# Three eighths of the first feed-forward product as seven block products, in a written sequence

## The chip, the cores and the metric

One core of one Trainium2 chip runs the whole kernel. The metric is device time in microseconds (us) of one execution. Engines: TensorE (PE) multiplies, VectorE (DVE) and ScalarE (ACT) prepare and evict, GpSimd (POOL) does little, SyncE (SP) issues the loads. Each engine takes its instructions in the order in which they stand in its own queue; semaphores tie the queues together.

## The reference

A residual block of a streaming encoder: a retention branch and a latent-attention branch, merged by gates, then a squared-ReLU MLP. Everything is float32; 256 rows (SEQ), model width 2048, hidden width 8192. The change touches the MLP alone:

```python
z = _rmsnorm(h, norm_mlp_g[l]) @ w_up[l]          # 256 x 2048 by 2048 x 8192
h = h + jnp.square(jax.nn.relu(z)) @ w_down[l]    # 256 x 8192 by 8192 x 2048
return _rmsnorm(h, norm_f_g)
```

## The kernel before

Every float32 operand is split in two float32r halves, `hi` (ScalarE rounds it, L151 for weights, L216 or L219 for activations) and `lo = raw - hi` (VectorE, L152, L217 or L220). A product is the sum of hi·hi, hi·lo and lo·hi in PSUM. Weights arrive by SyncE in 512 KB tiles `raw` (five buffers), and give `hi` and `lo` (four buffers each).

There are two forms of product. A *transposed unit* (`t_unit`, L170) holds a 128 x 128 block of weights stationary and streams the activations: for each of 16 blocks along the contraction one matmul of 512 columns (L159: x hi and x lo side by side) and one of 256 (L163: weight lo by x hi). Its 128 outputs by 256 rows lie in one PSUM bank in two halves, which `joined` adds (L206 copies one half by ScalarE, L207 adds by VectorE). The *normal form* (`n_tile`, L196, and `down`, L807) holds the activations stationary and streams 512 columns of weights, three matmuls for each block: L199, L200, L202, or L814, L815, L816.

The MLP runs in three stages. In the stage `wo` (L770) the merged branches are multiplied with `w_out`; 512 columns at a time are added to `hn`, and `mlp_turn` (L757) transposes them through PSUM (L764) and splits them into `hT`. In the stage `up` (L785 to L800) 64 transposed units give `z`; L800 squares the positive part into `hid`, which stays in SBUF. In the stage `dn` (L802 to L838) each of 64 blocks of `hid` is split into `dh` and `dl` (three buffers each, L820 to L822) and multiplied with two 512 KB halves of `w_down` into eight PSUM banks; L840 to L863 add, normalise and store.

PSUM has eight banks of 512 float32 columns, four under the tag `mm` and four under `at`. Within a stage the order of the instructions on each engine is set by the framework's scheduler from costs that it assumes; the program's order is only its input.

Of the kernel before, what the change touches and what calls it, by code (L numbers as in the profile page):

```python
# [27 lines left out]
CHUNK = 64  # L28
DFF = 8192
FT = DFF // P  # L30
EPS = 1e-6
QK_SCALE = float(192.0 ** -0.5)
LOWEST = -3.4e38
# [55 lines left out]
def block_kernel(ctx: ExitStack, tc: tile.TileContext, A):  # L89
    nc = tc.nc  # L90
    V, SC, G, PE = nc.vector, nc.scalar, nc.gpsimd, nc.tensor
# [3 lines left out]
    cp = ctx.enter_context(tc.tile_pool(name="cp", bufs=1))  # L95
# [4 lines left out]
    def big(name, dt=F32, shape=(P, KT, S)):  # L100
        return act.tile(list(shape), dt, tag="act16", name=name)
# [31 lines left out]
    def mmps(name):  # L133
        return pmm.tile([P, 512], F32, tag="mm", name=name)
# [4 lines left out]
    uid = [0]  # L139
# [15 lines left out]
    HK = KT // 2  # L155
# [40 lines left out]
    def n_tile(out, w, x, t, k0, nk, start, stop):  # L196
# [4 lines left out]
        for k in range(nk):  # L201
            PE.matmul(out, x.hi(k0 + k, ts), w[1][:, k], start=False, stop=stop and k == nk - 1)  # L202

    def join(out, ps):
        t = sm.tile([P, S], F32, tag="join", bufs=2, name="join")
        SC.copy(t, ps[:, S:])  # L206
        V.tensor_tensor(out=out, in0=ps[:, :S], in1=t, op=ALU.add)  # L207

    def joined(ps):
        t = sm.tile([P, S], F32, tag="val", bufs=2, name="val")  # L210
        join(t, ps)
        return t

    def split(hi, lo, val, scale=None):
        if scale is None:
            SC.copy(hi, val)  # L216
            V.tensor_tensor(out=lo, in0=val, in1=hi.bitcast(F32), op=ALU.subtract)  # L217
# [12 lines left out]
    warm = cp.tile([P, 1], F32, name="warm")  # L230
    SC.activation(warm, halfpi, AF.Copy)

    cold = cp.tile([P, 512], BF16, name="cold")
# [5 lines left out]
    rctx = ExitStack()  # L239
    rope_pool = rctx.enter_context(tc.tile_pool(name="rope", bufs=2))  # L240
    ictx = ExitStack()
    ip = ictx.enter_context(tc.tile_pool(name="ip", bufs=1))

# [8 lines left out]
    x = Pair("x")  # L252
# [97 lines left out]
    rxb = cp.tile([P, S], F32, name="rxb")  # L350
    V.tensor_copy(rxb, pb[:, :S])

    tabs = []
# [1 line left out]
    def table(j):  # L355
        ang, kk = angs[j]
        sgn = vec[:, V_INV + 2 + j : V_INV + 3 + j]
        own = ip if j == 0 else cp
        cos = own.tile([P, S], F32, name=f"cos{j}")
        sin = own.tile([P, S], F32, name=f"sin{j}")  # L360
# [157 lines left out]

    with ExitStack() as mctx:
        cc = big("cc", F32R, shape=(P, 2 * LT, 2, S))  # L520
        kpe = cp.tile([P, S], F32, name="kpe")
        lp = ExitStack()
        lpool = lp.enter_context(tc.tile_pool(name="lp", bufs=1))

# [230 lines left out]
    hT = Pair("hT")  # L755

    def mlp_turn(c):  # L757
        for jj in range(2):
            pT = atps(f"ht{c}{jj}")
            for j in range(2):  # L760
                kt = 4 * c + 2 * jj + j
                for t in range(2):
                    o = j * S + t * P
                    PE.transpose(pT[:, o : o + P], hn[:, t, kt * P : (kt + 1) * P], ident)  # L764
                g = vec[:, V_MLP + kt : V_MLP + kt + 1]
                split(hT.hi(kt), hT.lo(kt), pT[:, j * S : (j + 1) * S], scale=g)
    hp = ctx.enter_context(tc.tile_pool(name="hp", bufs=1))
    ssh = cp.tile([P, 2, 4], F32, name="ssh")
    rh2 = cp.tile([P, 2], F32, name="rh2")
    for c in range(4):  # L770
        cs = slice(c * 512, (c + 1) * 512)
        pss = [mmps(f"wo{c}{t}") for t in range(2)]
        for kq in range(4):
            n_unit(pss, A["w_out"][4 * c + kq], mg, 4 * kq, 4, kq == 0, kq == 3)
            if kq == 0 and c:
                mlp_turn(c - 1)
        for t in range(2):
            V.tensor_tensor(out=hn[:, t, cs], in0=pss[t], in1=hn[:, t, cs], op=ALU.add)
            SC.activation(pss[t], hn[:, t, cs], AF.Square, accum_out=ssh[:, t, c : c + 1])
# [2 lines left out]
    V.tensor_scalar(rh2, rh2, 1.0 / D, EPS, op0=ALU.mult, op1=ALU.add)  # L782
    V.reciprocal(rh2, rh2)

    up = [mmps(f"z{i}") for i in range(2)]  # L785
    for i in range(2):
        t_half(up[i], A["w_up"][i], hT, 0)
        if i == 0:
            mlp_turn(3)
    hid = [big(f"hid{i}") for i in range(3)]  # L790
    hid.append(hp.tile([P, KT, S], F32, name="hid3"))
    for i in range(FT):
        if i < 2:
            pz = up[i]
            t_half(pz, A["w_up"][i], hT, 1)
        else:
            pz = mmps(f"z{i}")
# [5 lines left out]
    ssf = cp.tile([P, 2, 68], F32, name="ssf")  # L803
    rf = cp.tile([P, 2], F32, name="rf")
    LAST = 2

    def down(i, t, c, w, hs):  # L807
        (hi, lo), (dh, dl) = w, hs
        ts = slice(t * P, (t + 1) * P)
        ws = slice(c % 2 * 512, c % 2 * 512 + 512)  # L810
        out = pd[t][c]
        end = i == FT - 1
        mm = tc.keep_in_program_order if i >= FT - LAST else (lambda ins: ins)
        mm(PE.matmul(out, dh[:, ts], hi[:, ws], start=i == 0, stop=False))  # L814
        mm(PE.matmul(out, dh[:, ts], lo[:, ws], start=False, stop=False))  # L815
        mm(PE.matmul(out, dl[:, ts], hi[:, ws], start=False, stop=end))  # L816

    tail = []
    for i in range(FT):
        dh = hp.tile([P, S], F32R, tag="dh", bufs=3, name=f"dh{i}")  # L820
        dl = hp.tile([P, S], F32R, tag="dl", bufs=3, name=f"dl{i}")
        split(dh, dl, hid[i // KT][:, i % KT])  # L822
        ws = []
        for half in range(2):
            w = weights(A["w_down"][i][:, half * 1024 : (half + 1) * 1024], [P, 1024])
            ws.append(w)
            if i < FT - LAST:
                for t in range(2):
                    for c in (2 * half, 2 * half + 1):
                        down(i, t, c, w, (dh, dl))  # L830
        if i >= FT - LAST:
            tail.append((i, ws, (dh, dl)))
# [7 lines left out]
    def finish(t, c, lo, hi, n):  # L840
        h = hn[:, t, c * 512 + lo : c * 512 + hi]
        ps = pd[t][c][:, lo:hi]
        V.scalar_tensor_tensor(h, in0=ps, scalar=rh2[:, t : t + 1], in1=h, op0=ALU.mult, op1=ALU.add)
        junk = hp.tile([P, 512], F32, tag="junk", bufs=2, name=f"junk{t}{n}")
# [32 lines left out]
def _t_units(w):  # L877
    k, n = w.shape
    return np.ascontiguousarray(w.reshape(k // P, P, n // P, P).transpose(2, 1, 0, 3))


def _n_units(w):
    k, n = w.shape
    u = w.reshape(k // 512, 4, P, n // 512, 512).transpose(3, 0, 2, 1, 4)
    return np.ascontiguousarray(u.reshape(-1, P, 4, 512))


def _cols(v):
# [57 lines left out]
```

## Time and profile before

| | |
|---|---|
| median of three runs | 1631.6 us (1631.03 to 1631.93) |
| the profiled execution | 1632.22 us, span 1630.4 us, granted clock 0.998 |
| PE busy, of the span | 1614.9 us (99%) |
| DVE, ACT, POOL busy | 996.2 us (61%), 809.7 us (50%), 49.5 us (3%) |
| moved by DMA | 304.46 MB, mean 187 GB/s |
| stage `wo` | from 825.4 us |
| stage `up` | 915.3 to 1272.5 us |
| stage `dn` | 1272.5 to 1621.0 us |

Matmuls are pipelined: the duration of one overlaps that of the next, so what a matmul costs is read from the distance of the starts, not from its mean duration. PEld is the load of the stationary operand, which runs beside the matmuls. A wait in the profile names the engine and line that released it.

### The profile page before, as it was taken

Reading aid. Unit: us, or ns where it says so; the run is one execution under the profiler, and the core shown is the slowest. Engines: PE = TensorE matmul, PEld = TensorE weight load, DVE = VectorE, ACT = ScalarE, POOL = GpSimd, SP = SyncE. Lnnn points to the kernel's source line nnn. Section 1 sums busy time; section 2 is a strip of 40 time slices with the busy share of each in tenths; the row PEclk is TensorE's granted clock in tenths of the full one; section 3 lists DMA queues with packets and bytes.
Section 4 is the critical chain, followed back from the end, with each engine's and each line's share of the span. In section 5 each row is a group of like instructions: output and inputs, shape, how many; then the busy total and the mean of one; then the engine's idle time right before and its main releaser. Section 6 shows DMA issues by size and latency. Waiting matters only on the chain.

```text
span 1630.4 us, 23041 instructions
## 1 busy us (share of the span) xinstructions
PE 1614.9 (99%) x8782; PEld 1398.8 (86%) x8782; DVE 996.2 (61%) x1491; ACT 809.7 (50%) x1249; POOL 49.5 (3%) x62
## 2 busy tenths in 40 slices
PE   8999999999999999999999999999999999999997
PEld 6888888888889889888888888888888888888886
DVE  7974588655556658666765555555555555555555
ACT  6544555544445556765545544444444444444444
POOL 7100000000000000000000000000000000000001
PEclk9999999999999999999999999999999999999999
DMA  8665544555556554325575555555555655555553
GB/s 306 200 233 193 187 156 166 169 192 186 190 170 203 190 191 146 125 94 176 186 246 187 174 193 188 192 189 186 191 192 184 223 194 192 193 193 195 192 194 112
DMA packets 84480, 304.46 MB, mean 187 GB/s; under 512 B 9360, under 2 KB 9488, under 8 KB 83600
## 3 DMA queue, kind: packets, MB, share of 16 engines
q1 hardware_dynamic: 84368, 302.98, 55.3%
q8 instruction: 69, 1.13, 0.3%
q14 instruction: 43, 0.35, 0.1%
HBM read 300.84 MB, written 2.10 MB: 186 GB/s over the span
## 4 chain that ended last, share of the span: by engine, by line
PE 97%; DVE 1%; issue 0%; DMA 0%; ACT 0%; POOL 0%; SPq 0%; DVEq 0%; POOLq 0%; ACTq 0%
PE z L159 14%; PE z L163 8%; PE dn L816 7%; PE dn L814 7%; PE dn L815 7%; PE rg L159 4%; PE yr L159 4%; PE gr L159 4%; PE gm L159 4%; PE mo L159 4%; PE qk L159 2%; PE gr L163 2%; PE yr L163 2%; PE gm L163 2%; PE rg L163 2%; PE mo L163 2%
## 5 line engine op out<-in xcount | busy, mean ns | idle before, releaser
L152 DVE TENSOR_TENSOR lo<-raw,hi 128x1024 fp32r<-128x1024 f32 (+2 forms) x562 | 666.0, 1204 | 521.6 <-ACT hi L151 248.3
L151 ACT CAST hi<-raw 128x1024 fp32r<-128x1024 f32 (+2 forms) x562 | 580.8, 1035 | 536.9 <-PE z L159 135.2
L159 PE MATMUL z<-hT,hi 128*128 128x512 f32 x1024 | 245.5, 391 | 0.0
L159 PEld LDWEIGHTS z<-hT,hi 128*128 128x128 f32 x1024 | 188.0, 188 | 36.1
L815 PE MATMUL dn<-lo,dh 128*128 128x512 f32 x512 | 199.2, 389 | 0.0
L816 PE MATMUL dn<-hi,dl 128*128 128x512 f32 x512 | 199.2, 389 | 0.0
L814 PE MATMUL dn<-hi,dh 128*128 128x512 f32 x512 | 198.9, 389 | 0.0
L163 PEld LDWEIGHTS z<-hT,lo 128*128 128x128 f32 x1024 | 131.6, 191 | 5.1
L163 PE MATMUL z<-hT,lo 128*128 128x256 f32 x1024 | 133.1, 283 | 0.0
L815 PEld LDWEIGHTS dn<-lo,dh 128*128 128x128 f32 x512 | 96.1, 188 | 20.1
L816 PEld LDWEIGHTS dn<-hi,dl 128*128 128x128 f32 x512 | 96.1, 188 | 19.9
L814 PEld LDWEIGHTS dn<-hi,dh 128*128 128x128 f32 x512 | 96.1, 188 | 19.8
L216 ACT CAST dh<-hid 128x256 fp32r<-128x256 f32 x64 | 26.0, 407 | 89.3 <-PE dn L815 89.3
L159 PE MATMUL mo<-my,hi 128*128 128x512 f32 x256 | 65.5, 396 | 0.4 <-DVE val L207 0.4
L159 PE MATMUL rg<-x,hi 128*128 128x512 f32 x256 | 64.0, 395 | 0.0
L159 PE MATMUL yr<-ry,hi 128*128 128x512 f32 x256 | 61.4, 391 | 0.0
L159 PE MATMUL gr<-x,hi 128*128 128x512 f32 x256 | 61.3, 391 | 0.0
L159 PE MATMUL gm<-x,hi 128*128 128x512 f32 x256 | 61.1, 391 | 0.0
L159 PEld LDWEIGHTS gm<-x,hi 128*128 128x128 f32 x256 | 47.0, 188 | 9.1
L159 PEld LDWEIGHTS gr<-x,hi 128*128 128x128 f32 x256 | 47.0, 188 | 9.0
L159 PEld LDWEIGHTS yr<-ry,hi 128*128 128x128 f32 x256 | 46.9, 188 | 9.0
L159 PEld LDWEIGHTS rg<-x,hi 128*128 128x128 f32 x256 | 46.2, 188 | 8.6
(271 smaller groups left out, 2239.1 us busy)
## 6 DMA issues: line engine op xcount, KB each, us to landing
raw<-w_up SPq DMA_DIRECT2D x128, 512.0 KB, 4.2
raw<-w_down SPq DMA_DIRECT2D x128, 512.0 KB, 4.3
raw<-w_rv SPq DMA_DIRECT2D x32, 512.0 KB, 4.5
raw<-w_rg SPq DMA_DIRECT2D x32, 512.0 KB, 4.5
raw<-w_gret SPq DMA_DIRECT2D x32, 512.0 KB, 4.3
raw<-w_ret_o SPq DMA_DIRECT2D x32, 512.0 KB, 4.6
raw<-w_gmla SPq DMA_DIRECT2D x32, 512.0 KB, 4.4
raw<-w_out SPq DMA_DIRECT2D x32, 512.0 KB, 3.7
```

The costliest lines, as they stand in the source:

```text
L151: SC.copy(hi, raw)
L152: V.tensor_tensor(out=lo, in0=raw, in1=hi.bitcast(F32), op=ALU.subtract)
L159: PE.matmul(out, w[0][:, k], x.both(k0 + k), start=start and k == 0, stop=False)
L163: PE.matmul(out[:, :S], w[1][:, k], x.hi(k0 + k), start=False, stop=stop and k == n - 1)
L216: SC.copy(hi, val)
L814: mm(PE.matmul(out, dh[:, ts], hi[:, ws], start=i == 0, stop=False))
L815: mm(PE.matmul(out, dh[:, ts], lo[:, ws], start=False, stop=False))
L816: mm(PE.matmul(out, dl[:, ts], hi[:, ws], start=False, stop=end))
```

## The change

The first 3072 of the 8192 columns of `w_up` (`SU = 3` blocks of 1024, 24 of the 64 units) are computed in the normal form by a scheme with seven block products in place of eight. In each of 8 *steps* of a block (`SJ`), a 256 x 256 piece of the activations (two row blocks by two contraction blocks) meets a 256 x 1024 piece of the weights (two by two blocks). Four of the seven stationary operands are differences of activation blocks (`Combos`, made four times, twice in `wo` and twice in `up`); four of the seven streamed operands are sums of weight blocks (`forms`, made on VectorE in each step). A step has four parts, with 2, 2, 2 and 1 products of three matmuls of 512 columns. The seven sums stay in seven PSUM banks through the 8 steps of a block; then `s_end` combines them on ScalarE and VectorE into `zo`, and four `turn`s of four transposes each bring them into the layout of `hid`.

The other 40 transposed units stay. Three stand first, two last, and 35 lie between the parts of the steps, each in two halves: one after part 3 of every step but the last, one after part 1 of every second step. They and the turns share the one PSUM bank that a block leaves free. The stage is written out for five engines (`manual_schedule`): weights are loaded seven parts and split four parts ahead of the matmuls.

`hid` goes to DRAM: each unit or turn is evicted by ScalarE (copy or ReLU, square) into one of four `hs` buffers, stored by SyncE, and in the stage `dn` loaded again by GpSimd's queue into one of three `hl` buffers (a pair of blocks, 256 KB). `hn` is stored to DRAM in the stage `up` and loaded back as `hn2`. The stage `dn` takes the 40 units' blocks first. Some small tiles move to other pools.

```diff
+SU = 3
+SJ = KT // 2
+EARLY, LATE = 3, 2
+AHEAD = 4
+MAKE = 7, 2 * EARLY + 18
+SUMS = (4, 7, 10), (0, 1, 2)
...
+    PRODUCTS = ((3, 0, 0), (4, 0, 1), (2, 1, 0), (5, 1, 1), (6, 2, 0), (1, 2, 1), (7, 3, 0))
+    class Combos:
...
+        def make(self, c):
...
+            x, q = wtile("raw", [P, 2, 2, 2, P]), wtile("raw", [P, 2, 4, P])
+            hi, lo = self.pair.span(4 * c, 4)
...
+            V.tensor_tensor(out=xs, in0=hi.bitcast(F32), in1=lo.bitcast(F32), op=ALU.add)
...
+            V.tensor_tensor(out=a2, in0=a11, in1=a12, op=ALU.subtract)
+            V.tensor_tensor(out=a5, in0=a11, in1=a21, op=ALU.subtract)
+            yield
+            V.tensor_tensor(out=a6, in0=a2, in1=a21, op=ALU.subtract)
+            V.tensor_tensor(out=a4, in0=a6, in1=a22, op=ALU.add)
+            yield
...
+            split(o[:, :, 0], o[:, :, 1], q)
...
+    class Step:
...
+            nc.sync.dma_start(self.ra, self.src[:, :2])
+            nc.sync.dma_start(self.rb, self.src[:, 2:])
...
+        def prep(self, part):
+            if part == 0:
+                V.tensor_tensor(
+                    out=self.fa, in0=self.rb[:, 1:].to_broadcast([P, 2, 512]), in1=self.ra, op=ALU.add
+                )
+            r = (self.ra, self.fa, self.fb, self.rb[:, :1])[part]
...
+            split(hi, lo, r)
+            self.ws[part] = hi, lo
+            if part == 0:
+                V.tensor_tensor(out=self.fb[:, 0], in0=self.fa[:, 0], in1=self.ra[:, 1], op=ALU.add)
+                V.tensor_tensor(out=self.fb[:, 1], in0=self.fb[:, 0], in1=self.rb[:, 0], op=ALU.add)
+        def mm(self, part):
...
+            for f, i, o in PRODUCTS:
+                if i == part:
+                    ah, al = self.x.get(f, self.j)
+                    q = self.qs[f]
+                    PE.matmul(q, ah, hi[:, o], start=first, stop=False)
+                    PE.matmul(q, al, hi[:, o], start=False, stop=False)
+                    PE.matmul(q, ah, lo[:, o], start=False, stop=last)
...
+    def s_end(qs, out, tmp):
...
+        SC.copy(t3, qs[3])
+        tt(V, e, qs[6], t3)
+        SC.copy(q5, qs[5])
+        tt(V, f, qs[2], e, ALU.subtract)
+        SC.copy(c12, qs[1])
+        tt(V, c21, qs[4], f)
+        SC.copy(c22, qs[7])
+        tt(V, c11, q5, f)
+        yield
+        tt(V, e, e, q5, ALU.subtract)
+        yield
+        tt(V, c12, c12, e)
+        yield
+        tt(V, c22, c22, t3)
+        yield
...
+        if c in (1, 2):
+            for _ in hc.make(c - 1):
+                pass
...
-    for i in range(FT):
-        if i < 2:
...
-            t_unit(pz, A["w_up"][i], hT)
-        z = joined(pz)
-        V.scalar_tensor_tensor(hid[i // KT][:, i % KT], in0=z, scalar=0.0, in1=z, op0=ALU.max, op1=ALU.mult)
+    hid = [hidd.tile([P, 2, S], F32, name=f"hid{i}") for i in range(FT // 2)]
...
+    def store(pair, n, t):
+        SC.activation(t, t, AF.Square)
+        later.append([3, lambda: nc.sync.dma_start(hid[pair][:, n : n + t.shape[1]], t)])
...
+        def evict(self):
+            pair, n = divmod(ST + self.i, 2)
+            t = zp.tile([P, 2, S], F32, tag="hs", bufs=4, name=f"hs{pair}{n}")
+            SC.copy(t, self.ps.rearrange("p (j n) -> p j n", j=2))
+            V.tensor_tensor(out=t[:, 0], in0=t[:, 0], in1=t[:, 1], op=ALU.add)
+
+            def rest():
+                SC.activation(t[:, :1], t[:, :1], AF.Relu)
+                store(pair, n, t[:, :1])
...
+    with tc.manual_schedule(engines=MANUAL):
+        for n, (it, h) in enumerate(parts):
+            ahead = AHEAD if n else 2
+            while loaded < min(len(parts), n + ahead + 3):
+                parts[loaded][0].load(parts[loaded][1])
+                loaded += 1
+            while prepped < min(len(parts), n + ahead + 1):
+                parts[prepped][0].prep(parts[prepped][1])
+                prepped += 1
+            it.mm(h)
+            if n == 0:
+                mlp_turn(3)
+                keep = hidd.tile([P, 2, D], F32, name="hnkeep")
+                SC.dma_start(keep, hn)
+                zo = big("zo", shape=(P, 2, 4, 512))
...
+    hn = big("hn2", shape=(P, 2, D))
+    nc.sync.dma_start(hn, keep)
...
-    for i in range(FT):
+    for n, i in enumerate((*range(ST, FT), *range(ST))):
+        if n % 2 == 0:
+            hl = hp.tile([P, 2, S], F32, tag="hl", bufs=3, name=f"hl{i}")
+            G.dma_start(hl, hid[i // 2])
...
-        split(dh, dl, hid[i // KT][:, i % KT])
+        split(dh, dl, hl[:, i % 2])
```

More of the change, by code (lines that the diff above doesn't have):

```diff
@@ L30 @@
 FT = DFF // P
+SU = 3
+SJ = KT // 2
+ST = SU * 1024 // P
+EARLY, LATE = 3, 2
+AHEAD = 4
+PAIRED = 6
+MAKE = 7, 2 * EARLY + 18
+SUMS = (4, 7, 10), (0, 1, 2)
+MANUAL = {getattr(mybir.EngineType, n) for n in ('Activation', 'DVE', 'PE', 'SP', 'Pool')}
+SSF = 68
 EPS = 1e-6
@@ new lines, in s_end, with tt @@
+    def s_end(qs, out, tmp):
+        t3, e, f, q5 = (tmp[:, i] for i in range(4))
+        c11, c12, c21, c22 = (out[:, t, c] for t in range(2) for c in range(2))
+        def tt(eng, o, a, b, op=ALU.add):
+            eng.tensor_tensor(out=o, in0=a, in1=b, op=op)
+        SC.copy(t3, qs[3])
[12 more added lines that the diff above has]
+        tt(V, c22, c22, t3)
+        yield
@@ L357, in table @@
         sgn = vec[:, V_INV + 2 + j : V_INV + 3 + j]
-        own = ip if j == 0 else cp
-        cos = own.tile([P, S], F32, name=f"cos{j}")
-        sin = own.tile([P, S], F32, name=f"sin{j}")
+        cos, sin = (
+            (ip if j == 0 else rope_pool).tile([P, S], F32, tag=f"{name}{j}", bufs=1, name=f"{name}{j}")
+            for name in ("cos", "sin")
+        )
         tc.keep_in_program_order(SC.activation(sin, ang, AF.Sin, scale=sgn))
@@ L764, in mlp_turn @@
                     PE.transpose(pT[:, o : o + P], hn[:, t, kt * P : (kt + 1) * P], ident)
+            for j in range(2):
+                kt = 4 * c + 2 * jj + j
                 g = vec[:, V_MLP + kt : V_MLP + kt + 1]
@@ new lines, in block_kernel, with square, __init__, load @@
+    forms = big("forms", shape=(P, 4, 2, 512))
+    later = []
+    def store(pair, n, t):
+        SC.activation(t, t, AF.Square)
+        later.append([3, lambda: nc.sync.dma_start(hid[pair][:, n : n + t.shape[1]], t)])
+    def square(pair, ps):
+        t = zp.tile([P, 2, S], F32, tag="hs", bufs=4, name=f"hs{pair}")
+        SC.activation(t, ps.rearrange("p (j n) -> p j n", j=2), AF.Relu)
+        store(pair, 0, t)
+    class Unit:
+        def __init__(self, i, order, between=None):
+            self.i, self.order, self.between, self.raw, self.ws = i, order, between, {}, {}
+        def load(self, part):
+            self.raw[part] = wtile("raw", [P, HK, P])
+            nc.sync.dma_start(self.raw[part], A["w_up"][self.i][:, part * HK : (part + 1) * HK])
+        def prep(self, part):
+            hi, lo = (wtile(kind, [P, HK, P]) for kind in ("hi", "lo"))
+            split(hi, lo, self.raw.pop(part))
+            self.ws[part] = hi, lo
+        def mm(self, part):
+            if part == 0:
+                self.ps = atps(f"z{self.i}")
+            w = self.ws.pop(part)
+            t_pass1(self.ps, w, hT, part * HK, HK, part == 0)
+            t_pass2(self.ps, w, hT, part * HK, HK, part == 1)
+            if part:
+                self.evict()
+            if self.between:
+                self.between(part)
+        def evict(self):
[6 more added lines that the diff above has]
+                store(pair, n, t[:, :1])
+            later.append([2, rest])
@@ new lines, in block_kernel, with turn, step, end @@
+    turns = []
+    def turn(u, jj):
+        pT = atps(f"zt{u}{jj}")
+        for j in range(2):
+            kt = 2 * jj + j
+            for t in range(2):
+                o = j * S + t * P
+                src = zo[:, 0, 2 * t + kt // 4, kt % 4 * P : kt % 4 * P + P]
+                PE.transpose(pT[:, o : o + P], src, ident)
+        square(4 * u + jj, pT)
+    def step(u, j, qs):
+        def end():
+            sums = s_end(qs, zo[:, 0].rearrange("p (t c) n -> p t c n", t=2), zo[:, 1])
+            next(sums)
+            later.extend([d, lambda: next(sums)] for d in SUMS[u == SU - 1])
+            turns.extend(lambda jj=jj: turn(u, jj) for jj in range(4))
+        def between():
+            if turns and j:
+                turns.pop(0)()
+        return Step(qs, A["w_up_s"][u, j], hc, j, between, end)
@@ new lines, in drain, with fn @@
+    def drain(n):
+        def fn(part):
+            for _ in range(n[part]):
+                turns.pop(0)()
+        return fn
+    early = [Unit(i, 0) for i in range(EARLY)]
+    parts = [(e, h) for h in range(2) for e in early]
+    units = list(range(EARLY, FT - ST - LATE))
+    slots = [(u, j, h) for u in range(SU) for j in range(SJ) for h in (1, 3)][:-1]
+    whole = [t for t in slots if t[2] == 3]
+    room = len(units) - len(whole)
+    halves = [t for t in slots if t[2] == 1]
+    if room >= 0:
+        use = set(whole) | {halves[i * len(halves) // room] for i in range(room)}
+    else:
+        use = {t for t in whole if t[1] != PAIRED or t[0] >= -room}
@@ new lines, in block_kernel @@
+    for u in range(SU):
+        qs = {}
+        for j in range(SJ):
+            st = step(u, j, qs)
+            for h in range(4):
+                parts.append((st, h))
+                if (u, j, h) in use:
+                    un = Unit(units.pop(0), 0)
+                    parts += [(un, 0), (un, 1)]
+    assert not units
+    for n, i in enumerate(range(FT - ST - LATE, FT - ST)):
+        un = Unit(i, 0, drain(((0, 1), (1, 2))[n]))
+        parts += [(un, 0), (un, 1)]
+    loaded = prepped = 0
@@ new lines, in block_kernel @@
+    making = iter(())
+    with tc.manual_schedule(engines=MANUAL):
[13 more added lines that the diff above has]
+                zo = big("zo", shape=(P, 2, 4, 512))
+            elif n in MAKE:
+                making = hc.make(2 + MAKE.index(n))
+            if n < 2 * EARLY or n % 2 == 0:
+                next(making, None)
+            for entry in list(later):
+                entry[0] -= 1
+                if entry[0] < 0:
+                    later.remove(entry)
+                    entry[1]()
+        while later:
+            later.pop(0)[1]()
```

91 lines of the change are left out of this document (67 added, 24 removed).

## The prediction

> **What bounds the kernel now.** First the head of the page and the shares of the chain that ended last, then the stretches of the two feed-forward stages, then the waits.
>
> ```profile
> span 1630.4 us, 23041 instructions
> PE 1614.9 (99%) x8782; PEld 1398.8 (86%) x8782; DVE 996.2 (61%) x1491; ACT 809.7 (50%) x1249; POOL 49.5 (3%) x62
> PE 97%; DVE 1%; issue 0%; DMA 0%; ACT 0%; POOL 0%; SPq 0%; DVEq 0%; POOLq 0%; ACTq 0%
> ```
>
> ```profile
> core 0: us, PE busy (x) PEld busy (x) DVE busy (x) ACT busy (x) POOL busy (x), PEclk, DMA share, GB/s
> 915.30:1272.50 357.20, 357.20 (x2057) 315.52 (x2056) 202.25 (x267) 162.44 (x203) 0.00 (x0) 1.00 0.56 189
> 1272.50:1621.00 348.50, 348.50 (x1539) 288.27 (x1537) 187.12 (x202) 155.47 (x202) 4.93 (x5) 1.00 0.56 187
> ```
>
> ```profile
> DVE lo L152 <- PE z L163: 145.1, 61, 3.0
> ACT hi L151 <- PE z L159: 135.2, 122, 1.6
> ```
>
> The chain is TensorE for 97% of the span. In the stage `up` (915.3 to 1272.5) and in `dn` PE is busy for the whole stretch, at full clock (1.00); VectorE works 202 of 357 us in `up`, ScalarE 162, and both wait for PE to free their buffers (145 and 135 us). So time goes only with PE work, in equal measure, and until another engine or a buffer makes PE wait. Since PE has no gap in `up`, a stall cannot be won back there: the costs below are bounded by nought from below.
>
> **PE work removed and added.** A transposed unit is priced by the distance of two far starts on the chain, a normal matmul by the first and last starts of `dn`, a transpose by four of them in `wo` and the matmul two places behind.
>
> ```profile
> 933.26 3.65 PE z L159 x16
> 1261.69 3.65 PE z L159 x16
> ```
>
> ```profile
> L814 PE MATMUL dn<-hi,dh x512: 389/389/396, 1272.7 to 1620.2; 128*128 128x512 f32 x171
> L816 PE MATMUL dn<-hi,dl x512: 388/389/389, 1273.1 to 1620.6; 128*128 128x512 f32 x171
> ```
>
> ```profile
> 852.74 0.60 PE L764 MATMUL ht<-con,hn 128*128 128x128 f32 x4
> 853.41 0.40 PE L200 MATMUL wo<-hi,mg 128*128 128x512 f32 x1
> ```
>
> Between 933.26 and 1261.69 lie 59 units of 5.567 us. `dn` has 3 x 512 matmuls: (1620.6 - 1272.7) / 1535 = 0.2266 us each. From 852.74 to 853.41 stand four transposes and one matmul: (0.67 - 0.23) / 4 = 0.11 us each. The change removes 24 units, 24 x 5.567 = 133.6 us. It adds 24 steps of 7 x 3 = 21 matmuls, 504 x 0.2266 = 114.2, and 3 x 16 transposes, 48 x 0.11 = 5.3. The sum is -14.1 us. Of this the seventh product saved is only a part (8 units hold 8 x 16 x 768 columns, 8 steps 168 x 512, seven eighths of it); the normal form also has 168 matmuls where the units have 256.
>
> The Trainium skill, "TensorE: Matmul & The Clock Gate", section "Wait — 56ns, not 53.3ns?", gives a warm matmul N / 2.4 GHz and about 2.5 ns. By that, as an estimate, a unit would take 5.20 us, a normal matmul 0.216, and the change would bring -10.7. The rows differ from it: 0.2266, and 0.348 for a pair of 512 and 256. I go by the rows.
>
> Without any stall the profiled time of 1632.2 us becomes 1618.1.
>
> **Work of the other engines in `up`.**
>
> ```profile
> L152 DVE TENSOR_TENSOR lo<-raw,hi 128x1024 fp32r<-128x1024 f32 x538 | 648.4, 1225 | 500.5 <-ACT hi L151 231.3 <-PE z L163 145.1 <-PE gr L163 36.1
> L217 DVE TENSOR_TENSOR dl<-hid,dh 128x256 fp32r<-128x256 f32 x64 | 27.2, 425 | 39.6 <-ACT dh L216 39.6
> L778 DVE TENSOR_TENSOR hn<-wo,hn 128x512 f32<-128x512 f32 x8 | 5.5, 688 | 1.0 <-PE wo L202 1.0
> ```
>
> ```profile
> L151 ACT CAST hi<-raw 128x1024 fp32r<-128x1024 f32 x538 | 565.1, 1052 | 513.3 <-PE z L159 135.2 <-PE dn L816 99.2 <-PE rv L200 43.2
> L216 ACT CAST ry<-sg 128x512 fp32r<-128x512 f32 x8 | 5.0, 620 | 3.6 <-DVE sg L488 3.6
> L425 ACT ACTIVATE sg<-sg 128x256 f32<-128x256 f32 x16 | 6.6, 412 | 0.0
> ```
>
> VectorE, for a step: four passes of 1024 columns (one sum, three `lo`) and three of 512: 4 x 1.225 + 3 x 0.69 = 6.97 us, against 4.76 of PE: 2.2 short. For a unit: 2 x 1.225 + 0.42 = 2.87 against 5.57: 2.7 to spare. ScalarE: 3 x 1.05 + 0.62 = 3.8 for a step, 2 x 1.05 + 0.62 + 2 x 0.41 = 3.5 for a unit. Over two steps with their three units PE has 26.2 us, VectorE 22.5, ScalarE 18.1 and two turns of 1.24. So PE stays the longest. In the first block VectorE also makes half the differences (2 x (2 x 1.225 + 4 x 0.425) = 8.3) and the first `dl` (1.3); with `s_end` (7 x 0.69 = 4.8) it has 8 x 6.97 + 12 x 2.87 + 14.4 = 104.6 us, against 8 x 4.76 + 12 x 5.57 = 104.9 of PE. That block has no reserve but the four parts (4.8 us of PE or more) that are split ahead. I take 1.5 us for it, nearer to the sums, which are level, than to the 6 of a half us at each of twelve evictions for which VectorE waits in its queue.
>
> In `wo` the two differences cost VectorE 4.15 and ScalarE 1.05 each, and two of five `raw` buffers. The waits for PE cover them, and three or more split tiles are ahead (12 x 0.2266 = 2.7 us of PE each): nothing, at most 2; with no cover 8.3.
>
> **Waits that are new.** The prices of transfers:
>
> ```profile
> raw<-w_up SPq DMA_DIRECT2D x128, 512.0 KB, 4.2
> out<-hn SPq DMA_DIRECT2D x8, 256.0 KB, 2.5
> con<-con SPq DMA_DIRECT2D x1, 256.0 KB, 13.4
> hn<-x SPq DMA_DIRECT2D x1, 2048.0 KB, 8.8
> ```
>
> First, the order of the changed kernel shows the splits of `hl24` (`dh24`, `dh25`, and their `dl`) not at `dn` but early in `up`, on ScalarE and VectorE ahead of the eviction of the fourth unit. They wait for the store of `hid12`, then for its load by GpSimd. Counted from the end of the third unit: ScalarE passes of 0.62, 0.82, 1.05 and 0.82 come before the last store (3.3 us), which lands after 2.5 (5.8), and the load after another 2.5 to 4.2 (8.3 to 10.0). ScalarE itself gets there at about 6.8. After the two splits it evicts the unit at 9.7 to 11.5; PE wants that bank at 2.7 + 5.6 + 2.0 = 10.3. No load by GpSimd's queue is in this trace: with the slowest row of 256 KB, 13.4, the eviction ends 10.4 us late. I take 1 us (0 to 10.4), nearest to the eight stores of 2.5. The Trainium skill, "DMA: Bandwidth & Descriptors", section "Anatomy of one DMA — SWDGE (gpsimd) path", has about 2.0 us and bytes over 436 GB/s for such a load, as an estimate 2.6 us, and by that PE would wait nothing. No run here shows it. `dh26` also moved forward, but stands behind two more units.
>
> Second, one PSUM bank serves 35 units and, in the second and third blocks, 8 turns. Where two parts of a step lie between two users, or more, PE has 2.0 us or more to be ahead of an eviction of 0.62. At twelve places, about the turns, it is one part of 1.36 us; if ScalarE has just begun a 1024-column pass, 1.05 + 0.62 - 1.36 = 0.3 us are lost. 0.5 us (0 to 4).
>
> Third, stores stand on SyncE between loads, and each waits for a square on ScalarE; behind it wait the loads for parts seven ahead. A load starts when a buffer is freed; from the pass that frees it to the pass that wants it VectorE has some 6 us of passes (3.7 where the differences hold two buffers) against the 4.2 of a load, and PE is four parts further behind: half a us at one place. `hn2` waits for PE's last use of the first differences, in the third block's fourth step; behind it two halves of a unit and the sixth step's weights, wanted 17 us of PE later, or about 8 before the four parts of lead. It moves 2 MB, 8.8 us when `hn` was loaded. 0.5 us (0 to 8.8). The store of `hn` at the start of `up` is the same size, and the loads for seven parts are out or queued: in the same price.
>
> Fourth, the boundary: the four `at` banks of `dn` come free after the last evictions, five ScalarE passes of 0.62 and one or two splits of 1.05, some 4 us; PE has transposes and twelve or more matmuls in the `mm` banks ready, 0.9 + 2.7. 1 us (0 to 3). Later in `dn` a pair's load is issued about four blocks (21.8 us) ahead of use, and 13.4 is covered: nothing. POOL's last work, at the end of the kernel, stands behind these loads, all issued well before: nothing.
>
> Together 1.5 + 1 + 0.5 + 0.5 + 1 = 4.5 us: 1618.1 + 4.5 = 1622.6 in the profiled execution. That one stood 0.6 above the median of its runs, so I predict 1622.0.
>
> **Rivals.** *VectorE bounds the first block.* For it: 104.6 against 104.9 us, with in-order waits for evictions, for two `raw` buffers held by the differences, and for `hl24`. Against it: the lead. Price: 6 and the `hl24` wait at 3 to 4, with 2.0 for the rest: 1618.1 + 11.5 - 0.6 = 1629.0. Chance 0.08.
>
> *Odd steps wait for their own preparation (slower).* An odd step has one unit only: 6.97 + 2.87 = 9.8 us of VectorE against 10.3 of PE. If the lead of four parts does not carry from unit to step (VectorE stands behind an eviction when it ought to split), each of the 12 odd steps shows its 2.2 us: 26.4, and the time is 1618.1 + 26.4 - 0.6 = 1643.9. It outweighs the gain from 1.2 us a step. For it: all seven sums and `lo` on the one engine. Against it: in the order the splits of four further parts stand ahead of each eviction, and a unit's eviction holds VectorE for 0.42. Chance 0.10.
>
> *Late loads of `hid` in `dn` (slower).* It decides from 21.8 us a load; at 25 us the 29 later pairs lose 3 each, 1618.1 + 87 - 0.6 = 1704.5. Nothing in the trace of 256 KB is over 13.4. Chance 0.03.
>
> *The steps save nothing.* The 504 matmuls would have to take (133.6 - 5.3) / 504 = 0.255 us; 1631.6. Both `wo` and `dn` run the form at 0.23. Chance 0.03.
>
> **The numbers.** The forecast has 0.76, its own range 1617.5 (no stall) to 1628. With the first rival the range is 1617.0 to 1630.5; the three others, 0.16, stay outside. A measurement of this kernel can tell about 0.2% (3.3 us) from no change: faster means under 1628.3, slower over 1634.9. Faster: 0.76 and half of the first rival, 0.80. Same: the other half and the last, 0.07. Slower: 0.13.
>
> **What would show it.** In the profile after, the stage `up` should last 343 to 350 us, with PE busy all but 2 to 8 us of it; starts of the step matmuls 0.227 us apart; VectorE busy about 296 us there (202 - 24 x 3.29 - 40 x 0.42 + 24 x 6.97 + 14.5 + 8.3), ScalarE about 260; one PE gap near the fourth unit; `dn` 348 us. I am wrong if PE gaps recur at each step with VectorE as releaser, if the gap at the fourth unit is over 5 us, or if `dn` grows.

## The result and the profile after

The changed kernel takes 1618.56 us (median of four runs, 1618.09 to 1619.12); the kernel before took 1631.76 us beside it. The ratio is 0.9920, with an interval of 0.9903 to 0.9937: 13.2 us, or 0.8%, are gained. The forecast was 1622.0, with 1617.0 to 1630.5. The profiled execution of the changed kernel took 1618.44 us (1632.22 before).

First the head of the page after, the shares of the chain that ended last, and the stretches of the stages `up` and `dn` (columns as before).

```profile
span 1616.7 us, 22933 instructions
...
PE 1601.8 (99%) x8566; PEld 1380.2 (85%) x8566; DVE 1089.9 (67%) x1568; ACT 889.2 (55%) x1393; POOL 67.4 (4%) x94
...
PE 97%; DVE 1%; DMA 0%; issue 0%; ACT 0%; POOL 0%; SPq 0%; DVEq 0%; POOLq 0%; ACTq 0%
```

```profile
914.70:1258.80 344.10, 344.10 (x1838) 296.73 (x1836) 289.86 (x333) 235.74 (x337) 2.43 (x4) 1.00 0.69 234
1258.80:1607.20 348.40, 348.40 (x1543) 288.48 (x1541) 185.72 (x200) 159.46 (x211) 19.91 (x33) 1.00 0.64 207
```

`up` went from 357.2 to 344.1 us, `dn` from 348.5 to 348.4. PE is busy in every microsecond of both, at full clock. Its starts say the same: from the start of `up` to the end of `dn` no matmul starts more than 0.32 us behind the one before it, as in the kernel before (0.31). VectorE went from 202 to 290 us in `up` and ScalarE from 162 to 236, beside PE. So the whole gain in these two stages is PE work that is no longer there, and there is no stall in `up`, nor at the boundary to `dn`. The boundary itself is not sharp: two matmuls of `dn` start at 1251.78, and eight transposes of the last block at 1258.72 or later. So sums over both stages are taken below from the first start of `up` to the last start of `dn`: 705.1 us before (915.47 to 1620.62) and 692.2 after (914.94 to 1607.15), 12.9 less.

The starts of PE's instructions around the fourth unit, from the timeline (start, duration):

```profile
932.56 0.40 PE L295 MATMUL zs<-hi,hT 128*128 128x512 f32 x1
932.79 0.40 PE L296 MATMUL zs<-hi,hT 128*128 128x512 f32 x1
933.02 0.39 PE L297 MATMUL zs<-lo,hT 128*128 128x512 f32 x1
...
934.85 0.39 PE L296 MATMUL zs<-shi,hc 128*128 128x512 f32 x1
935.08 0.39 PE L297 MATMUL zs<-slo,hc 128*128 128x512 f32 x1
935.30 1.98 PE L169 MATMUL z<-hT,hi 128*128 128x512 f32 x8
...
940.86 0.40 PE L295 MATMUL zs<-shi,hc 128*128 128x512 f32 x1
...
942.70 0.39 PE L297 MATMUL zs<-slo,hT 128*128 128x512 f32 x1
942.93 1.98 PE L169 MATMUL z<-hT,hi 128*128 128x512 f32 x8
```

The twelve matmuls of parts 0 and 1 take 935.30 - 932.56 = 2.74 us, the nine of parts 2 and 3 take 942.93 - 940.86 = 2.07: a step is 4.81 us, not the 4.76 of the prediction. The first ones behind a unit start 0.23 to 0.24 apart, the later ones 0.227. A unit between them is 5.56.

### The profile page after: what moved, and what is told of

The parts are those of the page before. It is cut to its first block, busy times and chain, and to the rows that moved or that the text cites. A ratio compares the mean times of both kernels' runs of the same rounds, so it can differ in the third digit from the quotient of the medians.

```text
span 1616.7 us, 22933 instructions
## 1 busy us (share of the span) xinstructions
PE 1601.8 (99%) x8566; PEld 1380.2 (85%) x8566; DVE 1089.9 (67%) x1568; ACT 889.2 (55%) x1393; POOL 67.4 (4%) x94
## 4 chain that ended last, share of the span: by engine, by line
PE 97%; DVE 1%; DMA 0%; issue 0%; ACT 0%; POOL 0%; SPq 0%; DVEq 0%; POOLq 0%; ACTq 0%
PE z L169 9%; PE dn L1067 7%; PE dn L1066 7%; PE dn L1068 7%; PE z L173 5%; PE rg L169 4%; PE yr L169 4%; PE gr L169 4%; PE gm L169 4%; PE mo L169 4%; PE zs L295 2%; PE zs L296 2%; PE zs L297 2%; PE qk L169 2%; PE gr L173 2%; PE yr L173 2%
## 5 line engine op out<-in xcount | busy, mean ns | idle before, releaser
L162 DVE TENSOR_TENSOR lo<-raw,hi 128x1024 fp32r<-128x1024 f32 (+2 forms) x434 | 514.5, 1200 | 366.2 <-ACT hi L161 238.2
L161 ACT CAST hi<-raw 128x1024 fp32r<-128x1024 f32 (+2 forms) x434 | 446.0, 1029 | 389.5 <-PE dn L1068 96.6
L169 PE MATMUL z<-hT,hi 128*128 128x512 f32 x640 | 159.5, 391 | 0.0
L169 PEld LDWEIGHTS z<-hT,hi 128*128 128x128 f32 x640 | 117.4, 188 | 22.6
L337 DVE TENSOR_TENSOR lo<-raw,hi 128x1024 fp32r<-128x1024 f32 x80 | 94.9, 1222 | 19.1 <-ACT hi L336 18.9
L173 PEld LDWEIGHTS z<-hT,lo 128*128 128x128 f32 x640 | 87.3, 190 | 6.2
L173 PE MATMUL z<-hT,lo 128*128 128x256 f32 x640 | 89.2, 282 | 0.0
L336 ACT CAST hi<-raw 128x1024 fp32r<-128x1024 f32 x80 | 80.4, 1049 | 7.4 <-PE wo L210 5.0
L336 ACT CAST shi<-forms 128x1024 fp32r<-128x1024 f32 x48 | 50.5, 1053 | 25.4 <-DVE forms L266 17.7
L337 DVE TENSOR_TENSOR slo<-forms,shi 128x1024 fp32r<-128x1024 f32 x48 | 58.2, 1221 | 4.9 <-ACT shi L336 4.9
```

Of the source, the lines that this page charges most:

```text
L161: SC.copy(hi, raw)
L162: V.tensor_tensor(out=lo, in0=raw, in1=hi.bitcast(F32), op=ALU.subtract)
L169: PE.matmul(out, w[0][:, k], x.both(k0 + k), start=start and k == 0, stop=False)
L173: PE.matmul(out[:, :S], w[1][:, k], x.hi(k0 + k), start=False, stop=stop and k == n - 1)
```

## The experiments

The question is how the gain comes about, and what kept all four stalls away that the prediction had priced. A stall is measured in two ways: by the idle time that a PE row shows before it, and by the distance of the step matmuls' starts above 0.227 us, since a matmul's row is 0.39 long and so hides some 0.16 us of each wait.

**The eighth product.** The same three blocks in the normal form with all eight products: no sums, no differences, no `s_end` but four copies.

```diff
-            for f, i, o in PRODUCTS:
...
+            k, c = ((0, 1), (1, 0), (1, 1), (0, 0))[part]
+            for t in range(2):
+                PE.matmul(q, ah, hi[:, o], start=first, stop=False)
+                PE.matmul(q, al, hi[:, o], start=False, stop=False)
+                PE.matmul(q, ah, lo[:, o], start=False, stop=last)
```

> The 24 steps do all eight block products in the normal form: no differences of activations, no sums of weights, no combination at the end (four PSUM banks are copied out by ScalarE), 24 matmuls a step for 21. Theory A, TensorE's own work sets the time and all else is covered: 72 more matmuls at 0.227 to 0.229 us, 16.4 us more than the changed kernel's 1618.6, so 1635, slower than the kernel before by 3. Rival C, the gain comes from the normal form, the written order or the spill and not from the eighth product saved: at most 1625. Rival B, VectorE's work is what holds the changed kernel: 1618 to 1622, since this one has 2.2 + 1.2 + ... some 4.5 us less VectorE work a step.

Measured 1634.27 us, ratio to the kernel before 1.0017 (1.0008 to 1.0026), no PE gap.

```profile
PE 1617.9 (99%) x8638; PEld 1394.6 (85%) x8638; DVE 967.3 (59%) x1403; ACT 847.1 (52%) x1341; POOL 67.5 (4%) x94
```

Theory A held. The kernel has 72 matmuls more than the changed kernel and 15.7 us more time (72 x 0.2266 = 16.3). From the first start of `up` to the last of `dn` it takes 708.5 us, 16.3 more than the changed kernel. So the product saved is the whole gain, and more: the normal form, the transposes, the written order and the way of `hid` through DRAM together lose 2.7 us.

**Two and four blocks.** Only `SU` is changed (2 and 4); for 2, units left over follow the last block.

> Two blocks of 1024 columns by seven products in place of three; the twelve units that find no place between parts stand at the end. Theory A: each block is worth a third of 13.2, 4.4 us, so 1623.0 (up to 1 more, as units at the end follow each other). Rival B, VectorE has no reserve in the first block and pays there: the loss sits in block one, the blocks are worth unequal amounts, and the time differs from 1623 by over 2.

> Four blocks in place of three; 32 units stay, 27 of them one after each step but four. Theory A: 4.4 us less again, 1614.2. Rival B, VectorE becomes the bound: 32 x 6.97 + 32 x 2.87 + 4 x 4.8 + 9.6 = 344 us of VectorE against 32 x 4.81 + 32 x 5.57 + 7 = 339 of TensorE, and with waits in its queue 345 to 355 for the stage: 1619 to 1629. I hold B for this kernel (TensorE gaps at the steps, released by VectorE).

Measured 1625.54 (ratio 0.9961, 0.9947 to 0.9975) and 1621.28 (0.9938, 0.9923 to 0.9952). Going by a third of the 13.1 us that `up` lost for each block, 1622.9 and 1614.2 would be due, so they lose 2.6 and 7.1. With four blocks the step matmuls' starts have 5.3 us more than in the changed kernel above 0.227, and three turns wait 0.6 to 0.7 each. The stretch of its first block, and PE's waits:

```profile
932.50:1037.50 105.00, 101.87 (x514) 85.07 (x513) 102.18 (x121) 73.05 (x103) 2.43 (x4) 1.00 0.66 222
```

```profile
PE zs L297 <- DVE slo L337: 2.8, 6, 1.0
PE zt L974 <- ACT hs L956: 2.0, 3, 0.7
```

VectorE is busy 102 of 105 us, and PE waits for its `slo`. For four blocks rival B held. With two blocks the time is over 2 us off, as rival B had it, but not by B's cause. There is one gap, 1.66 us, and the profile names VectorE as its releaser too; but ScalarE's and VectorE's rows ahead of it show what VectorE waited for:

```profile
968.58 0.50 PE L297 MATMUL zs<-slo,hc 128*128 128x512 f32 x1 [1.66 <-DVE slo L337]
```

```profile
965.92 0.41 ACT L336 CAST dh<-hl 128x256 fp32r<-128x256 f32 x1 [2.86 <-DMA hl<-hid]
```

```profile
966.36 0.43 DVE L337 TENSOR_TENSOR dl<-hl,dh 128x256 fp32r<-128x256 f32 x1 [2.97 <-ACT dh L336]
```

Both engines stood at the early split of a pair of `hid`, waiting for its load. By the starts this costs 1.9 of the 2.6 us; the rest shows no gap and stays open.

**One bank without its cover.** Units only behind part 3, two in a row after every second step, so that nothing lies between an eviction and the next user of the bank.

```diff
-                if (u, j, h) in use:
+                for _ in range(((u, j, 1) in use) + ((u, j, 3) in use) if h == 3 else 0):
```

> Units only behind whole steps: after every second step two units follow each other. Theory A with the single free PSUM bank as a cover that is needed: the second unit of each pair waits for the copy of the first, 0.59 us and some 0.1 of signalling, twelve times, 8 us: 1626 to 1627. Rival: the order of the units makes no difference, 1618.6.

Measured 1639.17, ratio 1.0047 (1.0032 to 1.0062): slower than before, and 20.6 us over the changed kernel where I had expected some 8. PE's rows with the largest and a usual gap, and its wait:

```profile
945.63 2.80 PE L169 MATMUL z<-hT,hi 128*128 128x512 f32 x8 [3.31 <-ACT hs L956]
...
1086.03 2.14 PE L169 MATMUL z<-hT,hi 128*128 128x512 f32 x8 [0.68 <-ACT hs L956]
```

```profile
940.00:950.00 10.00, 6.69 (x32) 5.69 (x31) 9.58 (x16) 3.71 (x6) 0.00 (x0) 0.84 0.58 182
```

Thirteen gaps of 0.68 to 3.31 us sum to 15.7. Eight are 0.68, the price that was expected for one. The other five sum to 10.3, because ScalarE had a cast ahead of the eviction. The first (3.31) is the eviction behind a `dh` split that waited 3.77 us for its load; after it the mean granted clock over ten us is 0.84 and the unit takes 1.7 us longer. Three (1.34 to 1.75) stand behind a cast that waited for VectorE's sum, and the last (2.58) behind one that waited 4.67 us for its weights. So the places with steps between two units are what hides the eviction; the order of the changed kernel is worth 20 us, more than its whole gain.

**How much VectorE work fits.** The first sum of a step is made twice (plus 9.3 us a block), three times (plus 18.6), and one 512-column sum twice (plus 5).

```diff
+                V.tensor_tensor(out=self.fa, in0=self.rb[:, 1:].to_broadcast([P, 2, 512]), in1=self.ra, op=ALU.add)
```

> The first sum of each step (fa, 128 x 1024, 1.22 us on VectorE) is computed a second time into the same tile; nothing else changes. Theory A (VectorE has a reserve in each block: 93 us busy of 105 in the first, 88 of 105.5 in the second; the passes overlap a little, a 1024-column pass adds about 1.16 us): plus 8 x 1.16 = 9.3 us a block leaves 102 of 105, PE shows no gap, 1618 to 1619.6. Theory B (the first block is level, as the prediction's sum of 104.6 against 104.9 us had it): the first block alone grows by 8 to 9 us, 1626 to 1628, with VectorE as releaser.

> The first sum of each step is computed three times. Theory A (reserve of some 12 us in the first block, 17 in the others): plus 18.6 us a block makes 111.6 of 105 in the first block, 106.5 of 105.5 in the others, less the lead of four parts: PE waits 4 to 8 us in the first block and 0 to 3 in all the others, 1623 to 1630. Theory B (level): the first block alone grows by 18, 1636 or more.

> Three blocks as in the changed kernel; the first 512-column sum of each step (fb, 0.69 us on VectorE) is computed twice, plus 8 x 0.63 = 5 us of VectorE a block. Repeating the sum of 1024 columns (plus 9.3 a block) cost 5.5 us, all in the first block. Theory A (the changed kernel has some reserve there, and the cost sets in between): 1618.6 to 1620. Theory B (the first block stands at its limit and the cost is in proportion): 1621 to 1622.

Measured 1624.07 (1621.74 to 1624.62), 1643.56 (1642.84 to 1645.82) and 1621.64 (1619.45 to 1622.97): 5.5, 25.0 and 3.1 us over the changed kernel. Its own three blocks, and the rows of gaps with the sum made twice:

```profile
932.50:1037.50 105.00, 105.00 (x553) 90.42 (x553) 92.97 (x108) 73.37 (x105) 2.43 (x4) 1.00 0.69 232
1037.50:1143.00 105.50, 105.50 (x560) 90.70 (x560) 87.88 (x98) 71.51 (x104) 0.00 (x0) 1.00 0.66 221
1143.00:1247.00 104.00, 104.00 (x553) 89.41 (x552) 86.17 (x97) 71.08 (x101) 0.00 (x0) 1.00 0.70 242
```

```profile
944.76 2.11 PE L169 MATMUL z<-hT,hi 128*128 128x512 f32 x8 [1.48 <-ACT hs L959]
961.91 0.50 PE L300 MATMUL zs<-lo,hT 128*128 128x512 f32 x1 [0.47 <-DVE lo L340]
964.37 0.50 PE L300 MATMUL zs<-slo,hc 128*128 128x512 f32 x1 [0.82 <-DVE slo L340]
992.77 0.50 PE L300 MATMUL zs<-slo,hc 128*128 128x512 f32 x1 [1.81 <-DVE slo L340]
```

By the sums the changed kernel has 12 us of VectorE's time free in its first block and some 18 in the others. My theory A took the 12 for a reserve; that is wrong for the first block, right for the others. With the sum made twice the time lies between the two theories, its loss in the first block as B had it; the 512-column sum made twice came out as theory B. Neither theory fits the sum made three times: A has 1630 at most, and B has the loss in the first block alone. Five more us already cost 3.1 (2.2 in the profiled execution), with one gap of 1.94 us at 989.00, in the step where the fourth making pass stands between the passes. The blocks without a making pass took 9.3 more us without a gap, and gave way only at 18.6, when all three blocks lost. The 1.48 us at 944.76 is once more the eviction behind a split that waited 4.65 us for its load.

**A shorter lead.** Split two parts ahead and load five ahead.

```diff
-AHEAD = 4
+AHEAD = 2
```

> AHEAD = 2 for 4: weights are split two parts ahead of the matmuls and loaded five ahead. Theory A (the lead covers the evictions for which VectorE and ScalarE stand in their queues): at the end of a unit only two parts of a step, 2.7 us of PE, are split; eviction 0.6 and 0.42, then 1.05 and 1.2 for the next split make 3.3, so 0.6 to 1 us is lost at some 24 to 35 places: 1633 to 1650, slower than the kernel before or level with it. Theory B (the reserve of VectorE is enough by itself): 1618.6 to 1621.

Measured 1630.56 (1628.18 to 1631.56), ratio 0.9991 (0.9982 to 1.0000): 12 of the 13.2 us are gone. Nine listed gaps of 0.21 to 1.09 us sum to 5.6; by the starts, step matmuls lose 9.4 us.

```profile
PE zs L297 <- DVE slo L337: 4.3, 6, 1.1
PE first L169 <- ACT hi L336: 3.5, 2, 2.8
```

(The second row is an earlier stage's, and stands in the changed kernel too.) The time is below theory A's 1633 to 1650, and theory B is refuted. The work of every engine is the same as in the changed kernel (VectorE 1089.3 us), so what is lost is lost by the shorter lead. But not all of it is VectorE on its way from unit to step: two of the gaps, 0.68 and 0.61 us at 954.58 and 955.92, stand behind the early split of `hid`, for whose load ScalarE waited 2.02 us. By the starts the first block loses some 5 us, at its second, fourth and fifth steps; the first steps of the other two blocks lose 1.7 each and their second steps 0.4.

**Sums on GpSimd.** Four blocks, with the two 512-column sums of a step moved.

```diff
-                V.tensor_tensor(out=self.fb[:, 0], in0=self.fa[:, 0], in1=self.ra[:, 1], op=ALU.add)
-                V.tensor_tensor(out=self.fb[:, 1], in0=self.fb[:, 0], in1=self.rb[:, 0], op=ALU.add)
+                G.tensor_tensor(out=self.fb[:, 0], in0=self.fa[:, 0], in1=self.ra[:, 1], op=ALU.add)
+                G.tensor_tensor(out=self.fb[:, 1], in0=self.fb[:, 0], in1=self.rb[:, 0], op=ALU.add)
```

> Four blocks for three (32 units in place of 40), and the two 512-column sums of each step (fb) on GpSimd in place of VectorE. VectorE loses 8 x 2 x 0.65 = 10.4 us a block. Theory A (VectorE's work was what cost the run with four blocks its gain, and GpSimd works beside it): no PE gap from VectorE, 1614 to 1616, faster than the changed kernel by 3 to 4.5 us. Theory B (GpSimd and VectorE hinder each other, a 512-column sum on GpSimd takes 1.42 us or more and VectorE's own passes grow by as much, or ScalarE waits for the later sum): 1619 to 1630, VectorE's mean pass longer than 1.22 us.

Measured 1661.2, ratio 1.0182 (1.0167 to 1.0197): 39.9 us over four blocks with all sums on VectorE, and worse than theory B had it. Groups by shape, of this kernel, from `up` on:

```profile
L281 POOL TENSOR_TENSOR forms<-forms,sraw 128x512 f32<-128x512 f32 x32 | 67.6, 2111 | 612.2 <-PE z L173 402.5 <-DVE forms L266 118.8 <-issue 77.5
L337 DVE TENSOR_TENSOR slo<-forms,shi 128x1024 fp32r<-128x1024 f32 x64 | 108.6, 1697 | 50.3 <-ACT shi L336 50.0
L336 ACT CAST shi<-forms 128x1024 fp32r<-128x1024 f32 x64 | 67.2, 1050 | 131.6 <-POOL forms L282 98.2 <-DVE forms L266 33.4
```

The sum that takes VectorE 0.69 us takes GpSimd 2.1 (1.26 where VectorE stood still), VectorE's `slo` pass grows from 1.22 to 1.70 us, and ScalarE waits 98 us for the sums. What VectorE gave up in work it lost in longer passes (it is busy for 1122.5 us, and 1123.4 with all sums on it), and the waiting comes on top. The Trainium skill, "SBUF — State Buffer", section "Who interferes with whom", says that a VectorE instruction with two inputs from SBUF gets in the way of a GpSimd instruction that reads SBUF; these rows agree.

**Can four blocks be had?** The third making pass moved into `wo`; that, and a lead of five parts; the lead alone. For the lead, the last part of a step has two buffers, and `hs` three.

```diff
-AHEAD = 4
+AHEAD = 5
-MAKE = 7, 2 * EARLY + 18
+MAKE = (2 * EARLY + 18,)
...
-        if c in (1, 2):
+        if c:
             for _ in hc.make(c - 1):
```

> Four blocks, and the third of the four making passes of Combos moved from the stage up into the stage wo, so that VectorE has about 4.1 us less to do in the first block, and two raw buffers are not held there. Theory A (the run with four blocks lost 3 us to VectorE in its first block; the rest, 2 us at the turns and some 0.2 a block, stays): 1617.5 to 1619, level with the changed kernel or up to 1 us faster. Theory B (VectorE is short in every block of four, and what is taken out of the first block shows up later, or wo pays for it): 1620 to 1622.

> As the one before, with AHEAD = 5 (weights split five parts ahead; two buffers for the last part of a step, and three hs buffers for four to make room). Theory A (a longer lead evens out VectorE's peaks): 1616 to 1618. Theory B (the sum of VectorE's work is what is short, which no lead changes, or evictions wait for a free hs buffer behind their stores): 1618 to 1624.

> Four blocks with the lead of five parts alone: the third making pass stays in the stage up, as in the changed kernel. Theory A (the lead evens out VectorE's peaks, and the 4.1 us of the pass moved to wo did little): 1616 to 1618, as the run with both. Theory B (the first block is short of VectorE in sum, 102 of 105 us busy with a lead of four, and needs both): 1619 to 1621.5, with PE gaps from VectorE in the first block alone.

Measured 1623.94 (1622.36 to 1624.50), 1616.51 (1616.22 to 1617.21; ratio 0.9910, 0.9896 to 0.9923) and 1623.46 (1622.02 to 1624.05). The two runs with one edit lie above the ranges of both their theories; the run with both is in theory A's. With both edits four blocks reach 14.8 us below the kernel before, against 13.2 for the changed kernel; all four of its runs lie below all four of that one's, but the two were not timed side by side, and the intervals of their ratios overlap.

Each edit alone seems to be worth nothing. It isn't so: both are held up by the load of `hid`. ScalarE's row, the PE rows and the stretch behind, first of the moved pass, then of the lead alone:

```profile
945.98 0.71 ACT L336 CAST dh<-hl 128x256 fp32r<-128x256 f32 x2 [5.92 <-DMA hl<-hid]
```

```profile
947.69 0.50 PE L295 MATMUL zs<-shi,hc 128*128 128x512 f32 x1 [2.06 <-ACT shi L336]
...
950.39 0.63 PE L297 MATMUL zs<-slo,hT 128*128 128x512 f32 x1
950.82 0.63 PE L295 MATMUL zs<-shi,hT 128*128 128x512 f32 x1
```

```profile
947.60:951.70 4.10, 3.49 (x9) 2.47 (x10) 4.03 (x5) 4.07 (x8) 0.00 (x0) 0.62 0.26 82
```

```profile
965.59 0.40 ACT L336 CAST dh<-hl 128x256 fp32r<-128x256 f32 x1 [8.09 <-DMA hl<-hid]
```

```profile
967.30:974.00 6.70, 5.91 (x14) 4.27 (x15) 6.70 (x8) 5.62 (x8) 0.00 (x0) 0.53 0.18 56
```

The first pair's split (in the one) and the second pair's (in the other) stand on ScalarE ahead of a cast that PE needs. PE waits 2.06 and 2.93 us, and then the granted clock is 0.62 and 0.53: the step matmuls start 0.43 us apart. By the starts this costs some 4.5 and 6.9 us. Without it the two would stand near 1619.4 and 1616.6: by this the lead is what four blocks needed, and the moved pass gave the lesser part. That is worked out from the starts, and not shown; no run took the load away. With both edits the first pair's load was as long (7.2 us), but ScalarE came to the split later and waited 0.69, and PE did not wait for it: three other gaps, 1.7 us together, are left there.

## Why the prediction was right

The direction and the range held, and so did the cause, PE work that is removed while the other engines keep up. How that work divides, and what the stalls cost, it had wrong. By its steps:

**PE work.** -14.1 us was forecast, and -12.9 measured, from the first start of `up` to the last of `dn`. Units, transposes and matmuls have the prices given; only the step was too cheap by 0.05 us, 1.2 over 24 steps, because the price was taken from `dn`, where nothing else stands between such matmuls. The Trainium skill's rate ("TensorE: Matmul & The Clock Gate", section "Wait — 56ns, not 53.3ns?") gave an estimate of -10.7, further off than the rows, as each of its prices is below the distance that the traces show. One reading was wrong: the product saved is not "only a part" of the gain. By the prediction's own prices eight products would take 576 x 0.2266 + 5.3 = 135.8 us for the units' 133.6, so the form alone loses 2.2; the run lost 2.7.

**The stalls: 4.5 us, measured 0.** This is the mis-sized term. For the profiled execution 1622.6 was forecast and 1618.44 measured, 4.2 less: 4.5 of stalls that did not come, 1.2 for the step the other way, and 0.8 that lies ahead of `up` and behind `dn`. (`up` starts between 914.0 and 915.5 us in the fourteen traces, so part of a microsecond between two of them need not come from the change.) The median is 3.4 below its forecast: this profiled execution stood 0.1 below its median, where 0.6 above was assumed.

- *First block on VectorE, 1.5 taken.* No gap. The 104.6 us of work were 93.0 in that stretch: passes of 1.22 us start some 1.13 apart, so rows' durations count twice where they overlap, and five of the seven sums of `s_end` fall behind the block. Yet "level" was near the truth in another way: 5 us more cost 3.1, because work is not spread as in the sum.
- *The early split behind the load of `hid`, 1 taken, 0 to 10.4.* The wait is there, and PE misses it by half a microsecond:

```profile
938.19 0.78 POOL L1074 DMA_DIRECT2D hl<-hid  x1 [413.53 <-DMA hid<-hs]
```

```profile
941.25 0.71 ACT L336 CAST dh<-hl 128x256 fp32r<-128x256 f32 x2 [2.26 <-DMA hl<-hid]
941.87 0.58 ACT L956 COPY hs<-z 128x512 f32<-128x512 f32 x1
```

  The eviction ends at 942.45, PE wants the bank at 942.93. Counted from the end of the third unit (932.56), the load is in use at 8.7 us (8.3 to 10.0 forecast), the eviction ends at 9.9 (9.7 to 11.5) and PE wants the bank at 10.4 (10.3). So the chain of waits was forecast rightly; that it cost 0 and not 1 or more hung on half a microsecond, and is luck. The load took 3.1 us from its issue to its use. Three loads in other kernels took 4.2 (the sum made twice), 6.2 (the moved pass) and 7.9 (the lead alone), and cost about 1.5, 4.5 and 6.9 us. But a long load alone costs nothing: the second pair of the changed kernel took 8.2 us (954.68 to 962.85), ScalarE waited 1.76 for it, and PE not at all. The Trainium skill's fit, "DMA: Bandwidth & Descriptors", section "Anatomy of one DMA — SWDGE (gpsimd) path", gave 2.6 us; these five are all above it.
- *One bank, 0.5 taken.* Nothing, since steps lie between all its users. Without them there are 15.7 us of gaps.
- *Stores and `hn2`, 0.5; the boundary, 1.* PE has no gap at either. (In `wo` nothing was taken, and `up` starts 0.5 us earlier than before, not later.)

**Rivals.** That VectorE bounds the first block did not come about, but it is what stops the next step: it shows at four blocks, and at 5 us more work. That odd steps wait for their own preparation is refuted for the changed kernel. A lead of two parts loses 12 us, but not as the rival has it: four of the twelve odd steps lose 0.4 to 2.9 us, the other eight less than 0.1, and the first steps of two blocks, which are not odd ones, lose 1.7 each. So the splits that stand ahead of each eviction, the argument against this rival, do count. Late loads in `dn` and steps that save nothing are refuted by `dn`'s 348.4 us and by the eight products.

**What would show it.** `up` 343 to 350: 344.1. VectorE 296: 289.9. ScalarE 260: 235.7, for the same overlap of rows as on VectorE. PE gaps of 2 to 8 us, one near the fourth unit: none.

## What to carry to other kernels

When PE has no gap, price a change by PE's starts alone, and take the starts from a place with the same neighbours as the new one. A stall that is covered costs nothing, not its mean: ask of each wait what stands behind it in the queue and how many microseconds of split work PE still has, for it is the lead and the order that decide, not the sum of an engine's work. And look where an early, harmless-looking instruction of the next stage waits for memory in an in-order queue: the same kind of split cost from nothing to some 6.9 us, by the order around it.

## What the runs showed of the hardware

- The granted clock of PE is 1.00 or 0.50 in these traces, and in the stages `up` and `dn` it is halved for 3.4 us at a time (6.8 once). With the moved pass it is 0.50 from 948.55 to 951.97, behind 2.06 us of idle time; with the lead alone from 967.72 to 974.55, behind 2.93; the 0.62 and 0.53 above are means that hold these stretches. With units two in a row 3.31 and 2.58 us of idle time halved it. Idle times of 1.69 to 1.94 us left it at 1.00 in several kernels, but shorter ones did not always: 1.78 us halved it at 1275.44 with the sum made three times, and with the sums on GpSimd 1.02 us, two us behind a gap of 0.58, halved it at 1018.33. So no one length of gap decides; what does is not shown here. The Trainium skill, "TensorE: Matmul & The Clock Gate", section "What's actually happening", has the clock halved after an idle window of about 3.4 us; here less was enough.
- GpSimd and VectorE slowed each other: a 512-column sum on GpSimd went from 1.26 us to a mean of 2.1, a 1024-column pass on VectorE from 1.22 to a mean of 1.70.
- A 256 KB load by GpSimd's queue took from 2.9 us (the shortest) to 8.3 us (the longest) to land in these runs, where I had taken 2.5 to 4.2, and 13.4 at the worst.
